# Order of loads and side work in a layer kernel: later gains on half of h, temporaries in their own buffers, last gated block turned beside the down projection

## The chip, the cores and the metric

The kernel runs on one core of a Trainium2 chip (trn2). The metric is the device time of one execution in microseconds (us); lower is better. Each kernel is run several times, and the median counts. One further execution is profiled: the span, the rows and the busy times below are from that one.

## The reference

One layer with float32 inputs: x is 256 tokens of 2048 channels.

```
u = rms_norm(h, g_pre_mix)
proj = u @ w_in                                   # 2048 -> 5120
...   attention, convolution and recurrent groups, each normalised: mixed, 2048 wide
h = h + rms_norm(mixed @ w_out, g_post_mix)       # 2048 -> 2048
u = rms_norm(h, g_pre_ffn)
f = silu(u @ w_gate) * (u @ w_up)                 # 2048 -> 5632, twice
h = h + rms_norm(f @ w_down, g_post_ffn)          # 5632 -> 2048
```

rms_norm divides each token by its root mean square and multiplies channel by channel with a gain g. Products have float32's precision: each operand is split into a high part of the type fp32r and a low part, and three products (high by high, high by low, low by high) are added.

## The kernel before, in words

**Weights.** All weights go through one list, `stream`, of items. A standard item is 256 rows by 512 columns of a matrix (512 KB, `std`). Its way is: a DMA on SP's queue into a raw buffer (`load`, L252), a cast on ACT that makes the high part (`prep`, L274), a subtraction on DVE that makes the low part (L276), then the products on PE. Raw buffers are lent from the shelf `weights`: four (`NRAW`) at first, and three more, `xplaces[0]` to `xplaces[2]`, once the buffers in which x lay are free. There are five pairs of high and low tiles (`NPARTS`). When PE's products with an item have been written down, `release` counts it as done, and `top_up_one` prepares the next items for which a pair is free and then loads as many as it can, up to `AHEAD` = 6 items in front of the one prepared. The queues of PE, ACT and DVE keep the order in which the program writes their instructions. What SP and POOL issue is DMAs, each queue in its own order.

**Products.** A standard item makes 12 products of 512 columns (L333 to L335 in `product`, L326 to L328 in `six`): two halves of its rows, two token halves, three products each. In the feed-forward part the first 512 rows of a gate and an up block (items c0 and c1 of both, four quarters) are multiplied by a scheme of seven products of quarters in place of eight (`seven_in_turn`: P1, P6, P7, Q5, P2, R4, Q3), for all blocks but the first. An item of this scheme makes 6 products of 512 columns; its weights and its operands are sums of quarters, which DVE makes (`sums`, L259, for the weights; `forms` for h and f). P1, P6 and P7 are added up in one bank, and after each of the three ACT copies the value that the bank then holds (`ffn_after`, L1397), before PE may go on adding.

**Side work.** A `Side` job is a generator. After each item of the products one slot (`slot`) lets the jobs write down ACT, DVE and PE work for which their share has been saved up; `need(job)` runs slots until the job is done, which places all its work ahead of what follows.

**From h to the first gate.** The output projection's result makes h, four blocks of 512 channels by two token halves. `h_part` (L1099) adds it up, `h_turn` (L1105) transposes it on PE, `h_hi` (L1112 on DVE for blocks 2 and 3, and the cast L1115 on ACT) and `h_lo` (L1119, DVE) make the parts of it that PE multiplies. The first gate block runs in between, and the calls of `release` in that stretch say where the next weights' casts stand among this work. `h_job` then sums the squares of h on ACT (`squares`, L461), and the root of the mean follows. For blocks 0 and 1 of h the gain g_pre_ffn is not in h at first: the weights of the first gate and up block are multiplied by it instead (`late`, L270, L271). Later `regain_job(b)` multiplies h's block b by the gain: it adds high and low part (L1255, DVE), scales four quarters on ACT (L1258) and splits the result again (`split`: L1235 on ACT, L1236 on DVE); for b = 0 the operands of the seven products (`hform`) follow. Its temporaries h and s lie in `xplaces[0]` to `xplaces[2]`, and these go to the weights' shelf when it ends. Both jobs are added in front of the feed-forward loop, and the first product of block 1's gate asks for both (`side.need(*regain)` in `ffn_bank`). h is saved to memory by POOL's queue ahead of that (`hsave`, L1222).

**The feed-forward loop.** Eleven column blocks of 512; per block the gate items, then the up items. Block 0 has eight of each, c0 to c7; blocks 1 to 10 have the items c2 to c7 and the seven products of two blocks. P1, P6 and P7 of block i + 1 stand among the last up items of block i. When a gate block is complete `silu_job` makes its sigmoid (L1283) and gate values (L1286); `up_job` makes the gated values (L1294, L1295, L1299), transposes them on PE (L1306) and splits them into `fh` and `fl`, and for the four blocks in `SFORM` (1, 3, 5, 7) sends operands of the seven products to memory (`fsave`, L1323).

**The down projection.** After the loop `side.need(last_up)` writes down all that is left of the last block's `up_job`; then POOL loads the eight `fsave` tiles back (L1480), and `downs` runs: six standard items first, then items of seven products mingled with standard ones. `run` is the loop of both: bank, `six`, then `after`, `slot` and `release`.

Of the kernel before, what the change touches and what calls it, by code (L numbers as in the profile page):

```python
# [16 lines left out]
P = 128  # L17
D = 2048
S = 256
# [172 lines left out]
def block_kernel(ctx, tc, xT, x_tok, params, w_in, w_out, w_gate, w_up, w_down, lru_w, g_post, g_post2, out):  # L192
# [30 lines left out]
    for i in range(NFB):  # L223
        g, u = ([std(w[i, c], i=i, col=n, c=c, gains=None if i else late(c)) for c in range(2 if i else 0, 8)] for n, w in ((0, w_gate), (1, w_up)))
        if i:
            q = sevens[i]
            ffn += [*g[:2], q["Q5"], g[2], q["P2"], *g[3:5], q["R4"], g[5], q["Q3"]]
        if i == 0:
            q = sevens[1]
            ffn += [*u[:6], q["P1"], u[6], q["P6"], u[7], q["P7"]]  # L230
        elif i + 1 < NFB:
            q = sevens[i + 1]
            ffn += [*u[:-4], q["P1"], u[-4], q["P6"], *u[-3:-1], q["P7"], u[-1]]
        else:
            ffn += u
# [10 lines left out]
    at = {"load": 0, "prep": 0, "use": 0, "done": 0}  # L246
# [36 lines left out]
    def load_next():  # L283
        while at["load"] in early:
            at["load"] += 1
        i = at["load"]
        if i < min(len(stream), at["prep"] + AHEAD) and len(weights.free) >= len(stream[i].loads):
            load(i)
            at["load"] += 1
            return True  # L290
        return False

    def top_up_one():
# [10 lines left out]
        while load_next():  # L304
            pass
# [879 lines left out]
    release()  # L1185
# [6 lines left out]
    release()  # L1192
    release()
    r = rows(kh[8:10], [take()])
    for t in range(NT):
        half(acc[t], hidden, t, r)
    for t in range(NT):
        h_turn(t, 3)
        h_hi(t, 3)
        h_lo(t, 3)  # L1200
    for _ in range(5):
        release()
# [18 lines left out]
    for b in range(4):  # L1221
        G.dma_start(out=hsave[b], in_=xt[b])  # L1222
    ffp = ctx.enter_context(tc.tile_pool(name="ffp", bufs=1))
    fh, fl = ([place(ffp, f"f{n}{i}")(4, S, F32R) for i in range(NFB - 2)] +
              [place(xs, f"x1{2 * n + i}")(4, S, F32R) for i in range(2)] for n in range(2))
# [23 lines left out]
    def regain_job(b):  # L1249
# [3 lines left out]
        h = xplaces[b](4, S)  # L1253
# [7 lines left out]
        if b == 0:  # L1261
            s = xplaces[2](8, P)
# [6 lines left out]
            weights.free.append(xplaces[2])  # L1269
        weights.free.append(xplaces[b])  # L1270
# [18 lines left out]
    def up_job(i, acc):  # L1289
# [18 lines left out]
        turned = [b.rearrange("p (c t) -> p c t", c=4) for b in tps]  # L1308
        if i in SFORM:
# [23 lines left out]
    def part_tiles(x, k, t):  # L1333

        return [tuple(f(k + kk)[:, t * P:(t + 1) * P] for f in x) for kk in range(2)]

    def form_tiles(form, n):
        return [tuple(f[:, 2 * n + kk, :] for f in form) for kk in range(2)]
# [8 lines left out]
    def run(seq, uses, bank_of, after, tail=0):  # L1347
# [7 lines left out]
        for n, (item, to, tiles) in enumerate(order):  # L1355
# [5 lines left out]
            six(bank, tiles, ws[item], n == first[to], n == end[to] or item.name in READ, to in read)  # L1361
# [9 lines left out]
    def ffn_uses(item):  # L1371
# [3 lines left out]
        return [((item.i, *to), of_product(item.name, hidden, hform))]  # L1375

    def ffn_bank(item, to):
        if to not in accs:
            i, col, _ = to
            if i == 1 and col == 0:  # L1380
                side.need(*regain)
# [7 lines left out]
    def ffn_after(item, full):  # L1389
# [4 lines left out]
        if item.name == "P7":  # L1394
            dst = p167[i % 2]
        if dst is not None:
# [11 lines left out]
    regain = [side.add(1, regain_job(b)) for b in range(2)]  # L1408
# [65 lines left out]
    side.need(last_up)  # L1474
    spots = [stage[0], xplaces[3], place(hlp, "hl2"), place(hlp, "hl3"),
             *(place(ffp, f"hf{n}", 768) for n in range(2)), place(ffp, "p167"), place(ffp, "s")]
    for n, i in enumerate(SFORM):
        sforms[i] = [spots[2 * n + m](6, P, F32R) for m in range(2)]
        for m in range(2):
            G.dma_start(out=sforms[i][m], in_=fsave[i, m])  # L1480
# [17 lines left out]
    def down_uses(item):  # L1498
# [5 lines left out]
        return [((item.b + to[0], to[1]) if to else (item.b, item.name), of_product(item.name, x, sforms[item.i]))]  # L1504

    def down_bank(item, to):
        b, which = to
        half = b // 2
        if to not in ybanks:
            if item.name and half:  # L1510
                side.need(*yjobs[:2])
# [78 lines left out]
```

## Time and profile before

| what | value |
|---|---|
| time, three runs | 1086.96 us median (1086.84 to 1087.55) |
| time of the profiled execution | 1087.62 us |
| its span | 1085.9 us |
| PE busy | 1056.0 us, 97%, 4718 products |
| DVE busy | 849.8 us, 78% |
| ACT busy | 643.9 us, 59% |
| POOL busy | 21.9 us, 2% |
| DMA | 217.50 MB, 200 GB/s over the span |
| chain that ended last | PE 91%, DVE 3%, ACT 3%, issue 1%, DMA 1% |

The span runs from the first to the last instruction that the profiler recorded; 1.7 us of the execution's time lie around it. PE is TensorE's matmuls, PEld its weight loads, DVE VectorE, ACT ScalarE, POOL GpSimd, SP SyncE; SPq and POOLq are their DMA queues. The busy time of a product counts from its start to its modelled end, and products overlap; the pitch, from one start to the next, is what a product takes of PE's time. In a row of the timeline stand the start, the time, the engine, the line, the operation, what it writes and reads, and in brackets how long the engine had been idle before it and what it had waited for. "issue" is time in which the engine waited for nothing that the profile shows. The granted clock is given in parts of full speed.

### The profile page before, as it was taken

Reading aid. Unit: us, or ns where it says so; the run is one execution under the profiler, and the core shown is the slowest. Engines: PE = TensorE matmul, PEld = TensorE weight load, DVE = VectorE, ACT = ScalarE, POOL = GpSimd, SP = SyncE. Lnnn points to the kernel's source line nnn. Section 1 sums busy time; section 2 is a strip of 40 time slices with the busy share of each in tenths; the row PEclk is TensorE's granted clock in tenths of the full one; section 3 lists DMA queues with packets and bytes.
Section 4 is the critical chain, followed back from the end, with each engine's and each line's share of the span. In section 5 each row is a group of like instructions: output and inputs, shape, how many; then the busy total and the mean of one; then the engine's idle time right before and its main releaser. Section 6 shows DMA issues by size and latency. Waiting matters only on the chain.

```text
span 1085.9 us, 13088 instructions
## 1 busy us (share of the span) xinstructions
PE 1056.0 (97%) x4718; PEld 870.5 (80%) x4718; DVE 849.8 (78%) x1040; ACT 643.9 (59%) x819; POOL 21.9 (2%) x43
## 2 busy tenths in 40 slices
PE   8999999999999959999999999999999999999996
PEld 6788888888888748888888888888888788888885
DVE  5576998986687767888788788787786588888885
ACT  5778757678854655565556555555554355555562
POOL 0000001010000000000000000000000000000000
PEclk9999999999999999999999999999999999999998
DMA  8855554556563437566565575567668556646653
GB/s 294 290 185 173 191 175 156 192 171 212 195 234 116 174 118 243 180 207 216 189 224 192 188 232 194 188 210 249 201 200 293 180 194 204 228 172 222 223 191 117
DMA packets 62065, 217.50 MB, mean 200 GB/s; under 512 B 6832, under 2 KB 7216, under 8 KB 62000
## 3 DMA queue, kind: packets, MB, share of 16 engines
q1 hardware_dynamic: 58544, 206.18, 56.9%
q0 software_dynamic: 3456, 10.49, 2.8%
q8 instruction: 37, 0.61, 0.2%
q14 instruction: 28, 0.23, 0.1%
HBM read 209.30 MB, written 7.34 MB: 200 GB/s over the span
## 4 chain that ended last, share of the span: by engine, by line
PE 91%; DVE 3%; ACT 3%; issue 1%; DMA 1%; SPq 0%; DVEq 0%; ACTq 0%
PE acc L327 17%; PE acc L326 17%; PE acc L328 17%; PE acc L333 9%; PE acc L334 9%; PE acc L335 9%; PE bank L326 3%; PE bank L327 3%; PE bank L328 3%; DMA w<-xT 1%; DVE lo L276 1%; PE bank L1306 1%; PE bank L485 1%; ACT hi L274 1%; ACT junk L461 0%
## 5 line engine op out<-in xcount | busy, mean ns | idle before, releaser
L276 DVE TENSOR_TENSOR lo<-w,hi 128x1024 fp32r<-128x1024 f32 x419 | 509.2, 1224 | 188.6 <-ACT hi L274 181.0
L274 ACT CAST hi<-w 128x1024 fp32r<-128x1024 f32 x419 | 436.4, 1051 | 315.5 <-PE acc L328 136.7
L326 PE MATMUL acc<-hi,w 128*128 128x512 f32 x820 | 322.7, 394 | 8.1 <-issue 6.1
L327 PE MATMUL acc<-lo,w 128*128 128x512 f32 x820 | 321.7, 392 | 3.2 <-DVE lo L276 3.2
L328 PE MATMUL acc<-hi,w 128*128 128x512 f32 x820 | 321.6, 392 | 0.0
L326 PEld LDWEIGHTS acc<-hi,w 128*128 128x128 f32 x820 | 155.2, 189 | 41.1 <-issue 6.7
L327 PEld LDWEIGHTS acc<-lo,w 128*128 128x128 f32 x820 | 155.3, 189 | 35.7 <-DVE lo L276 3.9
L328 PEld LDWEIGHTS acc<-hi,w 128*128 128x128 f32 x820 | 155.2, 189 | 32.4
L333 PE MATMUL acc<-hi,w 128*128 128x512 f32 x336 | 134.7, 401 | 2.3 <-DVE w L471 1.1
L334 PE MATMUL acc<-lo,w 128*128 128x512 f32 x336 | 132.6, 395 | 1.1 <-DVE lo L276 0.8
L335 PE MATMUL acc<-hi,w 128*128 128x512 f32 x336 | 132.6, 395 | 0.0
L259 DVE TENSOR_TENSOR w<-w 128x1024 f32<-128x1024 f32 x72 | 87.7, 1218 | 0.0
L333 PEld LDWEIGHTS acc<-hi,w 128*128 128x128 f32 x336 | 63.8, 190 | 17.0 <-ACT hi L903 2.7
L334 PEld LDWEIGHTS acc<-lo,w 128*128 128x128 f32 x336 | 63.8, 190 | 15.3 <-DVE lo L276 1.6
L335 PEld LDWEIGHTS acc<-hi,w 128*128 128x128 f32 x336 | 63.7, 190 | 14.7 <-DVE w L1119 1.3
L326 PE MATMUL bank<-hi,w 128*128 128x512 f32 x168 | 65.4, 390 | 0.0
L327 PE MATMUL bank<-lo,w 128*128 128x512 f32 x168 | 65.4, 389 | 0.0
L328 PE MATMUL bank<-hi,w 128*128 128x512 f32 x168 | 65.4, 389 | 0.0
L727 DVE SCALAR_TENSOR_TENSOR w<-u,par,w 128x256 f32<-128x256 f32 x120 | 51.3, 487 | 0.0
L333 PE MATMUL acc<-hi,mh 128*128 128x512 f32 x128 | 50.5, 395 | 0.0
L335 PE MATMUL acc<-hi,ml 128*128 128x512 f32 x128 | 50.0, 390 | 0.0
L334 PE MATMUL acc<-lo,mh 128*128 128x512 f32 x128 | 49.9, 390 | 0.0
(259 smaller groups left out, 792.0 us busy)
## 6 DMA issues: line engine op xcount, KB each, us to landing
w<-w_gate SPq DMA_DIRECT2D x88, 512.0 KB, 3.7
w<-w_up SPq DMA_DIRECT2D x88, 512.0 KB, 4.2
w<-w_down SPq DMA_DIRECT2D x88, 512.0 KB, 4.4
w<-w_in SPq DMA_DIRECT2D x78, 512.0 KB, 3.4
w<-w_out SPq DMA_DIRECT2D x32, 512.0 KB, 3.5
fsave<-w POOLq DMA_DIRECT2D x8, 384.0 KB, 4.7
w<-fsave POOLq DMA_DIRECT2D x8, 384.0 KB, 5.4
w<-x_tok SPq DMA_DIRECT2D x4, 512.0 KB, 6.3
```

The source lines that it names most:

```text
L259: V.tensor_tensor(out=item.bufs[dst], in0=item.bufs[a], in1=item.bufs[b], op=op)
L274: A.copy(out=hi, in_=raw)
L276: V.tensor_tensor(out=lo, in0=raw, in1=hi.bitcast(F32), op=ALU.subtract)
L326: T.matmul(bank, xhi, hi[:, kk, :], start=first and kk == 0, stop=False, skip_group_check=again)
L327: T.matmul(bank, xhi, lo[:, kk, :], start=False, stop=False, skip_group_check=again)
L328: T.matmul(bank, xlo, hi[:, kk, :], start=False, stop=last and kk == 1, skip_group_check=again)
L333: T.matmul(acc, xh(k)[:, ts], hi[:, kk, :], start=first, stop=False)
L334: T.matmul(acc, xh(k)[:, ts], lo[:, kk, :], start=False, stop=False)
L335: T.matmul(acc, xl(k)[:, ts], hi[:, kk, :], start=False, stop=last)
L485: T.transpose(out=b[:, c * P:(c + 1) * P], in_=src[:, t, c * P:(c + 1) * P], identity=ident)
L727: V.scalar_tensor_tensor(out=cy[:, n, :], in0=u[:, n, j:j + S], scalar=pv("dw_conv_w", j * 4 + n), in1=cy[:, n, :], op0=ALU.mult, op1=ALU.add)
L1306: T.transpose(out=b[:, c * P:(c + 1) * P], in_=ss[t][:, c * P:(c + 1) * P], identity=ident)
```

## The change

Four parts:

- `at["ahead"]`: up to the feed-forward part an item is loaded only up to four ahead and one after each prepared item; from there on it is six ahead as before. With it SP's order at the start differs.
- The turn of h: the calls of `release` stand later, so blocks 2 and 3 of h come ahead of some weights. ACT's order from the first cast of block 2 on was cast, weight, cast, two weights, a weight pair with gains, the two casts of block 3, a pair with gains, squares; it is now two casts, two weights, the two casts of block 3, a weight, two pairs with gains, squares.
- The temporaries of `regain_job` lie in `ffp` tiles that are not yet in use (`f_place`), and `xplaces[0]` to `xplaces[2]` go to the weights' shelf as soon as h has been sent to memory. `regain_job(1)` is added only after block 1's P7, and only the items c2 and c3 of block 1 ask for it; these are now last among the items of each block from 1 on. `fh` and `fl` are made when a block is turned.
- `side.need(last_up)` is gone; the reloads on POOL are a side job of their own that waits for the last `up_job`, and the first seven-product item of the down projection asks for it.

```diff
     for i in range(1, NFB):
         sevens[i] = seven_in_turn(w_gate[i, 0], w_up[i, 0], w_gate[i, 1], w_up[i, 1], i=i)
     for i in range(NFB):
-        g, u = ([std(w[i, c], i=i, col=n, c=c, gains=None if i else late(c)) for c in range(2 if i else 0, 8)] for n, w in ((0, w_gate), (1, w_up)))
+        g, u = ([std(w[i, c], i=i, col=n, c=c, gains=None if i else late(c)) for c in ((4, 5, 6, 7, 2, 3) if i else range(8))] for n, w in ((0, w_gate), (1, w_up)))
         if i:
             q = sevens[i]
             ffn += [*g[:2], q["Q5"], g[2], q["P2"], *g[3:5], q["R4"], g[5], q["Q3"]]
...
     stream += downs[0] + downs[1]
     early = range(gate0 + 1, gate0 + 1 + NEARLY)
     parts = {}
-    at = {"load": 0, "prep": 0, "use": 0, "done": 0}
+    at = {"load": 0, "prep": 0, "use": 0, "done": 0, "ahead": NRAW}
 
     def load(i, raw=None):
         item = stream[i]
...
         while at["load"] in early:
             at["load"] += 1
         i = at["load"]
-        if i < min(len(stream), at["prep"] + AHEAD) and len(weights.free) >= len(stream[i].loads):
+        if i < min(len(stream), at["prep"] + at["ahead"]) and len(weights.free) >= len(stream[i].loads):
             load(i)
             at["load"] += 1
             return True
...
                 return False
             prep(i)
         at["prep"] += 1
-        while load_next():
+        while load_next() and at["ahead"] > NRAW:
             pass
         return True
 
...
     h_part(0, 3)
     h_lo(0, 2)
     h_part(1, 3)
-    release()
     half(acc[1], hidden, 1, r[4:7])
     h_turn(1, 2)
     half(acc[1], hidden, 1, r[7:])
     h_hi(1, 2)
     h_lo(1, 2)
     release()
-    release()
-    release()
     r = rows(kh[8:10], [take()])
-    for t in range(NT):
-        half(acc[t], hidden, t, r)
+    half(acc[0], hidden, 0, r)
     for t in range(NT):
         h_turn(t, 3)
+    half(acc[1], hidden, 1, r)
+    release()
+    for t in range(NT):
         h_hi(t, 3)
+    for t in range(NT):
         h_lo(t, 3)
-    for _ in range(5):
+    for _ in range(7):
         release()
 
     def h_job():
...
 
     for b in range(4):
         G.dma_start(out=hsave[b], in_=xt[b])
+    weights.free.extend(xplaces[:3])
+    at["ahead"] = AHEAD
     ffp = ctx.enter_context(tc.tile_pool(name="ffp", bufs=1))
-    fh, fl = ([place(ffp, f"f{n}{i}")(4, S, F32R) for i in range(NFB - 2)] +
-              [place(xs, f"x1{2 * n + i}")(4, S, F32R) for i in range(2)] for n in range(2))
+    fh, fl = {}, {}
+
+    def f_place(n, i):
+        return place(xs, f"x1{2 * n + i - NFB + 2}") if i >= NFB - 2 else place(ffp, f"f{n}{i}")
+
     both = place(ffp, "s")(NT, CB)
     ss = [both[:, t, :] for t in range(NT)]
     sums_f = both.rearrange("p t c -> p (t c)").rearrange("p (k t) -> p k t", t=P)
...
 
         while ("used", b) not in st:
             yield WAIT
-        h = xplaces[b](4, S)
+        h = f_place(b, 7)(4, S)
         yield 1.2, 0, 0
         V.tensor_tensor(out=h, in0=hh[b].bitcast(F32), in1=hl[b].bitcast(F32), op=ALU.add)
         yield 0, 2.0, 0
...
         yield 1.2, 1.05, 0
         split(hh[b], hl[b], h)
         if b == 0:
-            s = xplaces[2](8, P)
+            s = f_place(0, 8)(8, P)
             yield 1.9, 0, 0
             forms(s, *quarters(h))
             yield 1.0, 0.9, 0
             split(*hform, s[:, 2:8, :])
             yield 0.5, 0.4, 0
             split(hh[0][:, 0:2, P:], hl[0][:, 0:2, P:], s[:, 0:2, :])
-            weights.free.append(xplaces[2])
-        weights.free.append(xplaces[b])
 
     two = place(ffp, "p167")(2, CB)
     p167 = [two[:, 0, :], two[:, 1, :]]
...
+        fh[i], fl[i] = (f_place(n, i)(4, S, F32R) for n in range(2))
...
-        return [tuple(f(k + kk)[:, t * P:(t + 1) * P] for f in x) for kk in range(2)]
+        return lambda: [tuple(f(k + kk)[:, t * P:(t + 1) * P] for f in x) for kk in range(2)]
...
-            six(bank, tiles, ws[item], n == first[to], n == end[to] or item.name in READ, to in read)
+            six(bank, tiles(), ws[item], n == first[to], n == end[to] or item.name in READ, to in read)
...
     def ffn_bank(item, to):
+        if item.i == 1 and item.name is None and item.c < 4:
+            side.need(regain[1])
         if to not in accs:
             i, col, _ = to
             if i == 1 and col == 0:
-                side.need(*regain)
+                side.need(regain[0])
             if i:
                 side.need(*(added[n] for n in ((i - 1, 0),) if n in added))
                 while col and ("up", i - 1) not in st:
...
         dst = {"P1": p1, "P6": p16, "Q5": q5}.get(item.name)
         if item.name == "P7":
             dst = p167[i % 2]
+        if (i, item.name) == (1, "P7"):
+            regain.append(side.add(0, regain_job(1)))
         if dst is not None:
             A.copy(out=dst, in_=accs[(i, 1, 1) if item.name == "Q5" else (i, 0, 1)])
         if item.name == "Q5":
...
                     added[j, col] = side.add(0, job(j, [accs[j, col, t] for t in range(NT)]))
 
     added[0, 0] = side.add(0, silu_job(0, acc))
-    regain = [side.add(1, regain_job(b)) for b in range(2)]
+    regain = [side.add(1, regain_job(0))]
     run(ffn, ffn_uses, ffn_bank, ffn_after)
     last_up = added[NFB - 1, 1]
 
...
 
 
     sforms = {}
-    side.need(last_up)
     spots = [stage[0], xplaces[3], place(hlp, "hl2"), place(hlp, "hl3"),
              *(place(ffp, f"hf{n}", 768) for n in range(2)), place(ffp, "p167"), place(ffp, "s")]
-    for n, i in enumerate(SFORM):
-        sforms[i] = [spots[2 * n + m](6, P, F32R) for m in range(2)]
-        for m in range(2):
-            G.dma_start(out=sforms[i][m], in_=fsave[i, m])
+
+    def sforms_job():
+        yield 0, 0, 0
+        while last_up in side.jobs:
+            yield WAIT
+        for n, i in enumerate(SFORM):
+            sforms[i] = [spots[2 * n + m](6, P, F32R) for m in range(2)]
+            for m in range(2):
+                G.dma_start(out=sforms[i][m], in_=fsave[i, m])
+
+    sforms_ready = side.add(1, sforms_job())
     ff = of(fh, fl)
     NLAST = 4
     kept = {}
...
         to = {"P2": (0, 0), "Q3": (1, 0), "R4": (0, 1)}.get(item.name)
         four = [k for k in range(4 * item.i, 4 * item.i + 4)]
         x = [lambda k, f=f: f(four[k]) for f in ff]
-        return [((item.b + to[0], to[1]) if to else (item.b, item.name), of_product(item.name, x, sforms[item.i]))]
+        return [((item.b + to[0], to[1]) if to else (item.b, item.name), of_product(item.name, x, lambda: sforms[item.i]))]
 
     def down_bank(item, to):
         b, which = to
         half = b // 2
         if to not in ybanks:
-            if item.name and half:
-                side.need(*yjobs[:2])
+            if item.name:
+                side.need(*(yjobs[:2] if half else [sforms_ready]))
             if half == 0 and isinstance(which, int):
                 ybanks[b, 0], ybanks[b, 1] = acc_pair()
             elif half == 1 and not isinstance(which, int):
```

The first place is the start, SP's queue: `xT` is x, turned, by quarters of the channels (the first two in pieces), `w_in` the first weights. Before:

```order
L252 DMA w_179<-w_in 128x1024
L465 DMA w_148<-xT 128x512
L252 DMA w_182<-w_in 128x1024
L252 DMA w_192<-w_in 128x1024
L252 DMA w_194<-w_in 128x1024
L252 DMA w_196<-w_in 128x1024
L465 DMA w_204<-xT 128x1024
```

and now:

```order
L252 DMA w_179<-w_in 128x1024
L465 DMA w_148<-xT 128x512
L252 DMA w_182<-w_in 128x1024
L252 DMA w_192<-w_in 128x1024
L465 DMA w_200<-xT 128x1024
L252 DMA w_206<-w_in 128x1024
L252 DMA w_212<-w_in 128x1024
```

The third quarter of x stood behind four weights in a row and stands behind two now; the rest follows in the same alternation.

The second place is ACT's queue from the end of the first regain to the copies of block 1's P1, P6 and P7 (`w_3001` and `w_3002` are the high parts of h's blocks 0 and 1, the `hi` tiles weights, `par_72` the gains; `w_3477` and `w_3571` are the temporary of `regain_job(1)`, and the copies from `acc` are those of the three, L1397 before and L1405 now). Before:

```order
L1235 CAST w_3001<-w_3434 128x2x128
L1258 ACTIVATE w_3477<-w_3477,par_72 128x256 x4
L274 CAST hi_3501<-w_3461 128x1024
L1235 CAST w_3002<-w_3477 128x1024
L274 CAST hi_3525<-w_3410 128x1024
L1397 COPY w_3386<-acc_3531 128x512
```

and now:

```order
L1240 CAST w_3001<-w_3416 128x2x128
L274 CAST hi_3479<-w_3390 128x1024
L274 CAST hi_3497<-w_3388 128x1024
L1405 COPY w_3364<-acc_3501 128x512
L274 CAST hi_3509<-w_3392 128x1024
L274 CAST hi_3527<-w_3421 128x1024
L1405 COPY w_3365<-acc_3501 128x512
L274 CAST hi_3541<-w_3388 128x1024
L274 CAST hi_3561<-w_3463 128x1024
L1405 COPY w_3367<-acc_3501 128x512
L1263 ACTIVATE w_3571<-w_3571,par_72 128x256 x4
L1240 CAST w_3002<-w_3571 128x1024
```

The four scalings and the cast of the second regain stood ahead of the copy of P1, and now stand behind the copy of P7; each copy has two weights' casts ahead of it.

The third place is PE's queue at the end of the feed-forward loop (`bank` takes the transposes, `w_3383` and `w_3361` are the gated values). Before, with the last two up products first:

```order
L327 MATMUL acc_6668<-lo_6824,w_3004 128x512
L328 MATMUL acc_6668<-hi_6823,w_2904 128x512
L1306 MATMUL bank_6932<-ident_73,w_3383 128x128 x4
L1306 MATMUL bank_6937<-ident_73,w_3383 128x128 x4
L326 MATMUL acc_6962<-hi_6841,w_3361 128x512
```

and now:

```order
L326 MATMUL acc_6931<-hi_6875,w_4318 128x512
L327 MATMUL acc_6931<-lo_6876,w_4318 128x512
L328 MATMUL acc_6931<-hi_6875,w_4319 128x512
L1309 MATMUL bank_6978<-ident_73,w_3361 128x128 x4
L1309 MATMUL bank_6983<-ident_73,w_3361 128x128 x4
L326 MATMUL acc_6930<-hi_6893,w_4318 128x512
```

The transposes followed the last up product directly, and now stand behind three items of the down projection, 36 products; in front of these stands the last up product.

## Rows read from the trace of the kernel before

**Rows 1.** The page's slices: PE's busy tenths and its granted clock.

```profile
PE   8999999999999959999999999999999999999996
...
PEclk9999999999999999999999999999999999999998
```

**Rows 2.** Table of stretches: us, busy PE, PEld, DVE, ACT, POOL (instructions), clock, DMA share, GB/s.

```profile
375.00:400.00 25.00, 19.84 (x83) 15.51 (x82) 16.06 (x26) 14.81 (x24) 0.00 (x0) 0.97 0.38 126
400.00:425.00 25.00, 18.94 (x76) 15.02 (x75) 19.11 (x20) 15.06 (x21) 0.00 (x0) 0.82 0.58 187
```

**Rows 3.** PE's waits: for what, us in total, times, longest.

```profile
PE acc L326 <- issue: 6.1, 1, 6.1
PE acc L327 <- DVE lo L276: 3.2, 2, 2.2
PE bank L1306 <- DVE w L1299: 2.3, 1, 2.3
```

**Rows 4.** The start: SP's timeline, the chain that ended last, PE's timeline.

```profile
6.22 8.19 SPq L252 DMA_DIRECT2D w<-w_in  x4
...
14.46 6.07 DMA w<-xT
...
20.54 0.39 PE L335 MATMUL acc<-hi,w 128*128 128x512 f32 x1
...
28.71 0.39 PE L335 MATMUL acc<-hi,w 128*128 128x512 f32 x1
```

**Rows 5.** PE's timeline, the last nine products of the up projection, first and last.

```profile
839.76 0.39 PE L326 MATMUL acc<-hi,w 128*128 128x512 f32 x1
...
841.57 0.39 PE L328 MATMUL acc<-hi,w 128*128 128x512 f32 x1
```

**Rows 6.** Timeline, the turn of h and what precedes P1.

```profile
358.57 1.22 DVE L276 TENSOR_TENSOR lo<-w,hi 128x1024 fp32r<-128x1024 f32 x1
...
359.71 0.69 DVE L1112 TENSOR_TENSOR w<-bank,par 128x512 f32<-128x512 f32 x1
...
360.43 0.62 ACT L1115 CAST w<-w 128x512 fp32r<-128x512 f32 x1 [2.21 <-DVE w L1112]
...
368.85 1.33 ACT L270 ACTIVATE hi<-w,par 128x512 fp32r<-128x512 f32 x2
...
370.09 0.62 ACT L461 ACTIVATE junk<-w 128x512 f32<-128x512 f32 x1
...
390.87 1.99 ACT L274 CAST hi<-w 128x1024 fp32r<-128x1024 f32 x2
...
391.96 0.49 PE L326 MATMUL acc<-hi,w 128*128 128x512 f32 x1 [1.99 <-ACT hi L274]
```

**Rows 7.** Timeline, ACT and PE ahead of P6.

```profile
399.40 0.40 ACT L1235 CAST w<-w 128x256 fp32r<-128x256 f32 x1
...
402.25 1.70 ACT L1258 ACTIVATE w<-w,par 128x256 f32<-128x256 f32 x4 [2.46 <-DVE w L1255]
...
406.69 0.57 ACT L1397 COPY w<-acc 128x512 f32<-128x512 f32 x1
...
407.36 0.77 PE L326 MATMUL acc<-hi,w 128*128 128x512 f32 x1 [6.06 <-issue]
```

**Rows 8.** Table of stretches, behind the resumption at 407.36.

```profile
407.40:412.20 4.80, 4.80 (x12) 3.79 (x13) 4.76 (x5) 3.29 (x4) 0.00 (x0) 0.50 0.83 294
```

**Rows 9.** PE's timeline, the end of the gates.

```profile
844.22 1.29 PE L1306 MATMUL bank<-ident,w 128*128 128x128 f32 x8 [2.26 <-DVE w L1299]
...
845.27 0.47 PE L326 MATMUL acc<-hi,w 128*128 128x512 f32 x1
...
849.22 0.39 PE L327 MATMUL acc<-lo,w 128*128 128x512 f32 x1
```

**Rows 10.** The page's DMA issues: KB each, median us to landing.

```profile
w<-w_up SPq DMA_DIRECT2D x88, 512.0 KB, 4.2
...
w<-fsave POOLq DMA_DIRECT2D x8, 384.0 KB, 5.4
```

More of the change, by code (lines that the diff above doesn't have):

```diff
@@ L1333, in part_tiles @@
     def part_tiles(x, k, t):
-        return [tuple(f(k + kk)[:, t * P:(t + 1) * P] for f in x) for kk in range(2)]
+        return lambda: [tuple(f(k + kk)[:, t * P:(t + 1) * P] for f in x) for kk in range(2)]
     def form_tiles(form, n):
-        return [tuple(f[:, 2 * n + kk, :] for f in form) for kk in range(2)]
+        return lambda: [tuple(f[:, 2 * n + kk, :] for f in form()) for kk in range(2)]
     def of_product(name, x, form):
@@ L1374, in ffn_uses @@
         to = {"P2": (0, 0), "Q3": (1, 0), "Q5": (1, 1)}.get(item.name, (0, 1))
-        return [((item.i, *to), of_product(item.name, hidden, hform))]
+        return [((item.i, *to), of_product(item.name, hidden, lambda: hform))]
     def ffn_bank(item, to):
+        if item.i == 1 and item.name is None and item.c < 4:
+            side.need(regain[1])
         if to not in accs:
```

## Prediction, made before the changed kernel ran

> **What bounds the kernel now.** I read the slices first: PE is busy in nine tenths or more of nearly all of them, and at the full granted clock in nearly all [rows 1]. So the span is a row of products with a few holes, and a change is worth what it takes out of a hole. The table of stretches finds the widest: 19.84 and 18.94 us busy of 25 in the stretches from 375 and from 400 us, at mean clocks of 0.97 and 0.82 [rows 2]. The list of PE's waits says what ended them: once 6.1 us with no releaser that the profile could name, twice a weight's low part (3.2 us together), and, at another place, L1299's gated value in front of the last transposes (2.3) [rows 3]. A small hole lies at the start, between 20.54 and 28.71 us [rows 4].
>
> The pitch of products at full clock is 0.226 us: eight steps from 839.76 to 841.57 [rows 5]. A standard item is 12 products, 2.7 us; one of the seven is 6, 1.4 us.
>
> **Start: the later half of x goes ahead of two weights.** SP issues in its own order. Before, four weight loads took it 8.19 us from 6.22 on, since some waited for a raw buffer; only then, at 14.46, went the third quarter of x, which landed 6.07 later, at 20.53 [rows 4]. Now it stands behind two of these four. Spread evenly, the second ends at about 10.3 (an estimate from that row), and x lands at about 16.4, well before PE asks for it, at 20.77. From 20.54 to 28.71 PE made 27 steps in 8.17 us; at 0.226 they are 6.1. So at most **2.0 us** come back, and nothing if other transfers come late in its place. I take 1.9: the four microseconds won are twice the hole.
>
> The same edit, one load after each prepared item, leaves the rest of the first 340 us alone: every load still waits for the item that held its buffer, four back, and SP has the same loads in the same places. I cost it at nothing; the four raw buffers cover it.
>
> **The turn of h: the chain that leads to P1 starts earlier.** In front of P1 of block 1 stands one long chain on ACT and DVE: squares of h (from 370.09), root, sigmoid, gate values, first regain, P1's high part, which lets PE go on at 391.96 after a wait of 1.99 [rows 6]. From the first square to P1 that is 21.9 us, in the same order now as before, and nothing in it is removed. Its start moves. DVE made a weight's low part at 358.57 (1.22 us) before it came to L1112 at 359.71, and ACT's cast of the result stood until 360.43 [rows 6]. Now L1112 follows at 358.6 and the cast ends at 359.9. Then ACT has two weight casts (1.99 for two) to 361.9; DVE ends the second low part at 363.2 and two L1112 (0.69 each) at 364.6; ACT's second cast of that pair (0.62) ends at 365.2, one more weight cast at 366.2, two pairs with gains (1.33 each) at 368.8: there the squares start, in place of 370.09. So P1 comes **1.3 us** earlier. PE itself gets through the turn earlier too, but that buys a longer wait before P1, not time. Bounds: 0 (another wait in that chain) and 1.5.
>
> **Behind P1: the second regain leaves ACT's way.** P6 adds into the bank that P1 left, so it waits until ACT has copied P1's value. ACT's order was: a small cast at 399.40 (0.40), the four scalings of the second regain, which stood 2.46 for DVE (402.25, 1.70), a weight cast, the regain's cast, a weight cast, then the copy at 406.69 (0.57); PE resumed at 407.36, 0.1 later [rows 7]. This is the 6.1 that has no releaser. Now only two weight casts stand between the small cast and the copy: 399.80 + 1.99 + 0.57 + 0.1 = 402.5. So P6 starts **4.9 us** earlier, beside the 1.3 above. The most is the whole wait, 6.1; the least is 0, if the casts for c7 or P7 wait for their weights. These are loaded into the buffers freed early, as soon as the squares are done with them; the squares stand at the head of the 21.9 us chain, and a load takes some 4.2 [rows 10].
>
> The regain comes back behind the copy of P7. Its four steps are 1.2 + 1.7 + 1.0 + 1.2 = 5.1 us. Who waits for it is c2 of block 1's gate, which now stands behind c4, c5, Q5, c6, P2 and c7: 60 products, 13.6 us. That is the cover, and it exists only because c2 and c3 were put last; by itself their order moves nothing. Temporaries in another place cost nothing either.
>
> **The end of the gates: the last turn beside the down products.** The last up product is issued at 841.57; PE's next entry is the transposes at 844.22, 2.42 us late, and then, from 845.27 to 849.22, ten products take 3.95 us where 2.26 would do: 1.7 lost to a low clock [rows 5, 9]. In the new order the transposes stand behind three down items, 36 products or 8.2 us, and the gated values that they wait for come within 2.7 of the last up product. The three use blocks 0 and 2, long ready. The eight reloads on POOL come behind this, 5.4 us each from issue to landing [rows 10]; the seventh down item is the first that needs one, 16 us in. So **4.1 us** come back; 2.4 if the clock falls all the same.
>
> **Sum.** 1.9 + 1.3 + 4.9 + 4.1 = 12.2 us. The profiled execution took 1087.62, so 1075.4 for one like it; the median of the runs shown is 1086.96, 0.66 below, and the forecast on that scale is **1074.8**.
>
> **The clock.** After P6 the clock was at 0.50, its lower level of 1.2 GHz, for 4.8 us [rows 8]: 11 products, each 0.22 dearer, 2.4 us. It had fallen behind a run of waits and came back in unbroken work. I leave this loss in, since waits stand before P6 now too. PE was done with c6 at 401.3 (407.36 less 6.06); 1.3 earlier is 400.0, and P6 starts at 401.2 (402.5 less 1.3), so 1.2 us of slower products before P6 would not be felt.
> The Trainium skill ("TensorE: Matmul & The Clock Gate", section "HAM oscillation — how this bites in real kernels") speaks against the change here: waits of some microseconds between short groups of products put the array back to half rate each time, and the wait before P1 gets longer. By that rule all of c6 runs at half rate, up to 12 x 0.226 = 2.7 us dearer; 1.2 of it vanish as said, so its sum would lie between 1074.8 and 1076.3.
>
> **Rivals.**
> - *The clock comes back before P6* (chance 0.14). If it falls at P1 and rises again in c6's unbroken products, the 2.4 us of [rows 8] go too: 1072.4.
> - *The P6 stall only moves* (0.14): weights for c7 or P7 late, or the regain late for c2. For it: SP issues in order, so the load into the first x buffer, which waits for the squares, holds P1's weight behind it. Against it: nearly two thirds of the chain come after the squares. The 4.9 are lost: 1079.7.
> - *Start and turn give nothing* (0.08), as other transfers or casts take the place of those moved: 12.2 less 3.2 is 9.0, so 1078.0.
> - *Slower: the clock stays low* (0.03). Place: P6 to the end of block 1's gate, some 120 products. If all run at the lower level, 109 more than before at 0.226 each, they cost 24.6 us: 1099.4. It decides the sign from 54 products on (12.2 / 0.226). Against it: before, unbroken work brought the clock back within 4.8 us.
> The section of the Trainium skill named above shows a kernel whose clock fell back in every round; no run here shows that.
> - *No change* (0.03): the moved work lies off the path, 1087.0. Against it: the 6.1 us wait ends with ACT's copy to within 0.1.
>
> **How the numbers follow.** The forecast has 0.58, from 1073 to 1077. A measurement of this kernel tells 0.2% (2.2 us) from no change. Faster: 0.58 + 0.14 + 0.14 + 0.08 = 0.94; same 0.03; slower 0.03. The upper bounds, 2.0 + 1.5 + 6.1 + 4.4 (the last with transposes at full clock), make 1073.0; with most of the 2.4 the range starts at 1071.0. It ends at 1079.7.
>
> **What would show it.** In the profile after: no wait of PE between 20 and 29 us; P1 still behind a wait for ACT's cast, longer than 2.0; the 6.1 entry gone from PE's waits, or under 2; the last transposes without a wait and behind down products. It would be wrong if a new wait of over 2 us stood before P6, c2 or the first down items, or if the clock in the stretch from 400 us were below 0.82.

## The result and the profile after

The changed kernel takes 1072.21 us (median of 4 runs, 1072.03 to 1073.17), the kernel before 1087.26 (4 runs, 1086.84 to 1088.43): ratio 0.9862, 95% interval 0.9845 to 0.9879, 15.0 us less. The forecast was 1074.8 with a range from 1071.0 to 1079.7; the result lies inside the range, but below the 1073 to 1077 that the main forecast was given. The profiled execution took 1072.03, with a span of 1070.3.

The page of the kernel after, PE's busy tenths and its granted clock:

```profile
PE   8999999999999989999999999999999999999996
...
PEclk9999999999999989999999999999999999999998
```

The one weak slice of [rows 1], a 5, is an 8 now, and its clock is the one 8 in the middle. The table of stretches (us, busy time of PE, PEld, DVE, ACT and POOL with instructions, clock, DMA share, GB/s):

```profile
375.00:400.00 25.00, 19.82 (x68) 14.49 (x67) 18.74 (x28) 15.07 (x22) 0.00 (x0) 0.80 0.42 137
400.00:425.00 25.00, 25.00 (x116) 20.77 (x115) 22.04 (x23) 16.44 (x22) 0.00 (x0) 1.00 0.65 211
388.00:398.20 10.20, 8.42 (x18) 5.40 (x18) 9.83 (x14) 5.45 (x8) 0.00 (x0) 0.51 0.17 51
```

Against [rows 2] the second stretch is whole. In the first, PE is as busy as before with 68 products in place of 83, since the slow products lie here now: 18 of them between 388 and 398.2, at 0.51. PE's waits (for what, us in total, times, longest):

```profile
PE acc L326 <- ACT hi L274: 3.4, 1, 3.4
PE acc L327 <- DVE lo L276: 1.8, 2, 0.9
PE acc L333 <- DVE w L471: 1.5, 1, 1.5
```

Of [rows 3], the 6.1 without a releaser and the 2.3 in front of the transposes are gone. The longest now is P1's, 3.4 where it was 1.99 [rows 6]. The timeline of the kernel after, at the places of [rows 4 to 9]:

```profile
8.60 0.68 SPq L465 DMA_DIRECT2D w<-xT  x1
...
16.43 1.71 ACT L473 ACTIVATE w<-w,par 128x256 fp32r<-128x256 f32 x4 [0.21 <-DMA w<-xT]
...
26.57 0.39 PE L333 MATMUL acc<-hi,w 128*128 128x512 f32 x1
...
366.06 0.62 ACT L461 ACTIVATE junk<-w 128x512 f32<-128x512 f32 x1
...
384.15 1.71 ACT L1263 ACTIVATE w<-w,par 128x256 f32<-128x256 f32 x4 [3.74 <-DVE w L1260]
...
387.93 0.61 PE L326 MATMUL acc<-hi,w 128*128 128x512 f32 x1 [3.41 <-ACT hi L274]
...
397.56 0.57 ACT L1405 COPY w<-acc 128x512 f32<-128x512 f32 x1
...
397.67 0.63 PE L328 MATMUL acc<-hi,w 128*128 128x512 f32 x1
398.23 0.56 PE L326 MATMUL acc<-hi,w 128*128 128x512 f32 x1
...
830.27 0.39 PE L328 MATMUL acc<-hi,w 128*128 128x512 f32 x1
...
838.67 1.03 PE L1309 MATMUL bank<-ident,w 128*128 128x128 f32 x8
839.46 0.48 PE L326 MATMUL acc<-hi,w 128*128 128x512 f32 x1
```

Both kernels make the same products in the same number, so the start of the n-th can be compared: the lead of the kernel after, us. The last column gives what was gained since the row before that has an entry.

| product | before | after | lead | gained on the way |
|---|---|---|---|---|
| the 76th (third quarter of x well in use) | 28.94 | 26.57 | 2.4 | start 2.4 |
| at the end of the turn of h | 370.06 | 364.64 | 5.4 | |
| first of P1 | 391.96 | 387.93 | 4.0 | turn 1.7 |
| first of P6 | 407.36 | 398.23 | 9.1 | second regain 5.1 |
| in c7, both at full clock | 414.73 | 403.43 | 11.3 | clock 2.2 |
| last up product | 841.57 | 830.27 | 11.3 | |
| last of the products compared | 1075.21 | 1059.65 | 15.6 | end of the gates 4.3 |

### The profile page after: what moved, and what is told of

Same layout as the page of the kernel before. It is cut to its first block, busy times and chain, and to the rows that moved or that the text cites. A ratio compares the mean times of both kernels' runs of the same rounds, so it can differ in the third digit from the quotient of the medians.

```text
span 1070.3 us, 13089 instructions
## 1 busy us (share of the span) xinstructions
PE 1051.6 (98%) x4718; PEld 869.6 (81%) x4718; DVE 848.5 (79%) x1040; ACT 643.8 (60%) x819; POOL 21.8 (2%) x43
## 4 chain that ended last, share of the span: by engine, by line
PE 97%; DVE 1%; ACT 0%; issue 0%; DMA 0%; SPq 0%; DVEq 0%; ACTq 0%
PE acc L327 17%; PE acc L328 17%; PE acc L326 17%; PE acc L334 10%; PE acc L335 10%; PE acc L333 10%; PE bank L326 3%; PE bank L328 3%; PE bank L327 3%; PE bank L1309 1%; PE bank L485 1%; DVE w L1477 0%; PE bank L1105 0%; PE bank L795 0%; PE bank L846 0%
```

## The experiments

Four kernels each undo one part of the change, to see whether the gains of the table are each part's own. All are compared with the changed kernel's 1072.2; the kernel before stood at 1087.4 in those runs. In the later experiments it stood at 1087.6 and 1087.4. The changed kernel was not run again beside any of them, so differences of a few tenths say little. The traces have a noise of their own: by the 18th product, ahead of all that is changed but the start, one profiled execution is up to 1.8 us later than another. Where this matters it is taken off.

**The start undone.**

```diff
-    at = {"load": 0, "prep": 0, "use": 0, "done": 0, "ahead": NRAW}
+    at = {"load": 0, "prep": 0, "use": 0, "done": 0, "ahead": AHEAD}
```

> The changed kernel, with six loads ahead from the start on (the third quarter of x behind four weights again). Additive theory: PE's products get 2.25 us later by 28 us and stay so to the end, 1072.2 + 2.25 = 1074.5. Rival (the start's gain is taken up by a later wait, h's chain ending on something else): within 0.5 of 1072.2.

Measured: 1075.27 (1074.56 to 1075.82), 3.1 slower; in the traces the 74th product is 2.6 later and the end 2.9. SP's queue and ACT's first use of the third quarter:

```profile
6.32 7.86 SPq L252 DMA_DIRECT2D w<-w_in  x4
14.23 0.42 SPq L465 DMA_DIRECT2D w<-xT  x1
```
```profile
20.45 1.71 ACT L473 ACTIVATE w<-w,par 128x256 fp32r<-128x256 f32 x4 [4.65 <-DMA w<-xT]
```

The quarter goes 5.6 us later (14.23 for 8.60) and ACT starts on it 4.0 later. Nothing downstream takes the loss up. The loss is more than the 2.25 that was expected.

**The turn of h undone.**

```diff
     h_part(1, 3)
+    release()
     half(acc[1], hidden, 1, r[4:7])
...
     release()
+    release()
+    release()
     r = rows(kh[8:10], [take()])
-    half(acc[0], hidden, 0, r)
-    for t in range(NT):
-        h_turn(t, 3)
-    half(acc[1], hidden, 1, r)
-    release()
-    for t in range(NT):
-        h_hi(t, 3)
-    for t in range(NT):
-        h_lo(t, 3)
-    for _ in range(7):
+    for t in range(NT):
+        half(acc[t], hidden, t, r)
+    for t in range(NT):
+        h_turn(t, 3)
+        h_hi(t, 3)
+        h_lo(t, 3)
+    for _ in range(5):
         release()
```

> The changed kernel, with the releases in the turn of h where they stood. Additive theory: P1 of block 1 comes 1.8 us later and nothing else moves, 1074.0. Rival (the clock): with the turn undone PE's wait before P1 is about 2.0 again in place of 3.4, the clock stays up through P1 and falls only in c6, so that P6 and what follows run at 0.5 of the clock; 1.8 plus 2 to 5 us, 1076 to 1079.

Measured: 1074.67 (1074.13 to 1075.47), 2.5 slower, 2.1 in the traces. The first square is at 368.24 in place of 366.06, and P1 2.2 later; nothing is lost behind it. But 0.5 of this was lost by the 18th product already, so the turn's own part is about 1.6 in the traces, as in the table. So the rival falls, and its reason with it: P1's wait is 2.0 again, as before the change, but the clock did not stay up until c6. The table of stretches has it low from 392.4 on, 2.3 us behind P1's start, and up again ahead of P6, which starts at 400.40:

```profile
390.10:392.30 2.20, 1.25 (x4) 0.84 (x5) 2.16 (x4) 0.90 (x1) 0.00 (x0) 0.98 0.00 0
392.40:399.20 6.80, 5.33 (x13) 3.71 (x12) 6.50 (x9) 3.45 (x5) 0.00 (x0) 0.51 0.23 77
```

**The second regain ahead of P6 again.**

```diff
-        if (i, item.name) == (1, "P7"):
-            regain.append(side.add(0, regain_job(1)))
...
-    regain = [side.add(1, regain_job(0))]
+    regain = [side.add(1, regain_job(b)) for b in range(2)]
...
-                side.need(regain[0])
+                side.need(*regain)
```

> The changed kernel, with the second regain's work ahead of the copy of P1 again, all else as changed. P1 as in the changed kernel (wait of 3.4). If the regain's 5.1 us in front of the copy are the whole of it: P6 5.1 later, 1077.3. If the earlier return of the clock hangs on this part too (a 5 us wait before P6 leaves the clock low behind it): another 1.9, 1079.2.

Measured: 1080.02 (1078.94 to 1081.66), 7.8 slower, more than the regain's own 5.1. The timeline in front of P6, and the table of stretches before and behind the wait:

```profile
404.45 0.57 ACT L1403 COPY w<-acc 128x512 f32<-128x512 f32 x1
...
405.12 0.77 PE L326 MATMUL acc<-hi,w 128*128 128x512 f32 x1 [7.32 <-issue]
```
```profile
395.30:397.80 2.50, 2.50 (x11) 1.71 (x10) 2.19 (x3) 1.35 (x2) 0.00 (x0) 1.00 0.61 208
405.20:411.20 6.00, 6.00 (x14) 4.74 (x15) 5.96 (x6) 3.25 (x4) 0.00 (x0) 0.50 0.53 184
```

P6 is 5.1 later by its own wait (the profiled execution, the slowest of the four, had lost 1.8 more among its first 18 products). The clock had come back in c6; in the wait it fell again, and 14 products behind it cost 2.7. So the earlier return of the clock in the changed kernel belongs to this part: without the long wait in front of P6 there is nothing for the clock to fall in a second time.

**The wait for the last turn restored.**

```diff
     sforms = {}
+    side.need(last_up)
```

> The changed kernel, with the wait for the last block's turn in front of the down projection again. Theory: 2.4 us of waiting, ten products and the transposes at half clock, 4.6 us in all, 1076.8. Rival (the clock falls in the first down products all the same, so only the wait counts): 2.4, 1074.6.

Measured: 1076.24 (1074.54, 1076.17, 1076.31, 1076.52), 4.0 slower. The profiled execution is the fastest of the four. The timeline at the transposes and the table behind them:

```profile
832.72 1.29 PE L1309 MATMUL bank<-ident,w 128*128 128x128 f32 x8 [2.26 <-DVE w L1302]
833.76 0.47 PE L326 MATMUL acc<-hi,w 128*128 128x512 f32 x1
```
```profile
834.00:838.00 4.00, 4.00 (x20) 3.26 (x19) 1.67 (x4) 1.64 (x2) 0.71 (x2) 1.00 0.89 300
```

The wait is that of [rows 9] to the hundredth, 2.26, and yet the clock stayed up. From the last up product to the end this execution loses 2.7 us: 2.4 of waiting, and 0.25 because the transposes take 1.04 to the next product in place of 0.79. That is not the clock: it was granted at 1.00 while they ran (832.60 to 833.80), as it was in the kernel before (844.20 to 845.20). The same kernel was profiled a second time.

> The kernel of u4_last_turn_waited once more, for a second profile: its first profiled execution was the fastest of four (1074.54), with the clock up behind the wait of 2.3 us, and the others were at 1076.2 to 1076.5. Theory: the clock falls behind this wait in some executions and not in others; in a slower one ten or so products behind the transposes have a pitch of 0.43 (1.7 to 2.2 us in all), in another like the first none has. Rival (the slower executions lose their time at another place): 1076 or more, with all products of that stretch at 0.23.

Measured: 1074.69, again a wait of 2.26, and again 20 products in 4 us at 1.00. The 2.7 us of wait and transposes are thus shown twice. That the other three executions lost their further 1.6 to 2.0 to the clock is likely: the mean granted clock over the span, which is on record for every execution, was 0.992 in the fastest and 0.990 in those three, and 0.002 of 1073 us is 2.1 us (an estimate, 1 to 3 by the rounding). Where in the kernel they lost it no profile shows. In the kernel before, the loss behind this wait is in [rows 9].

**c2 and c3 first again.**

```diff
-... for c in ((4, 5, 6, 7, 2, 3) if i else range(8))] ...
+... for c in (range(2 if i else 0, 8))] ...
```

> The changed kernel, with c2 and c3 first again in blocks 1 to 10. Theory: the second regain behind P7 is free only since c2 comes late. In the changed kernel its high part ends at 410.4 and its low part at 411.7, while the first gate item of block 1 starts at 403.9: with c2 there PE waits 6.5 us, 1078.7, and up to 2.7 more if the clock falls in the wait, 1081.4. Rival (the order of the items does nothing, since another item's weights could be taken meanwhile): within 1 of 1072.2.

Measured: 1081.76 (1081.06 to 1083.63), 9.6 slower. PE's timeline at block 1's first gate item and the table of stretches behind it:

```profile
410.77 0.80 PE L326 MATMUL acc<-hi,w 128*128 128x512 f32 x1 [6.51 <-ACT w L1240]
```
```profile
411.00:416.00 5.00, 4.96 (x12) 3.42 (x13) 2.12 (x2) 0.67 (x1) 0.00 (x0) 0.54 0.00 0
```

A wait of 6.51 and the clock behind it, the upper end of what was expected. Without the new order the part that gained 5.1 and brought the clock back would have lost all of that. That the order by itself moves nothing was not run.

**Products that keep PE awake.** Three kernels put extra products, whose result is read by nobody, into PE's waits (`FILL` says how many in front of which item; here the first kernel's):

```diff
+            if seq is ffn and n and order[n - 1][0] is not item:
+                for _ in range(FILL.get((item.i, item.name or item.c), 0)):
+                    T.matmul(filler, hh[3][:, 0, :P], hh[2][:, 0:2, :], start=True, stop=True, skip_group_check=True)
...
+    FILL = {(1, 'P1'): 15}
+    filler = banks.lend()
...
```

The first: the changed kernel, 15 in front of P1.

> The changed kernel with 15 products whose result nobody reads in front of P1, in PE's wait of 3.4 us, so that PE is not idle there. Theory: the clock stays up through P1 and c6, but P6 still starts when ACT has copied P1 (398.2), so the 17 slow products in front of it cost nothing: within 0.7 of 1072.2. Rival (the slow products are part of what sets the end, and the clock matters in itself): 0.2 for each of those behind the last wait in c6, 2.0 us, 1070.2.

Measured: 1073.62 (1071.46, 1072.52, 1074.72, 1074.81), 1.4 slower, which neither theory nor rival expected. In the profiled execution, the fastest, the clock stays up through P1 but falls in c6, behind a wait of 2.20:

```profile
388.00:393.00 5.00, 1.96 (x7) 1.34 (x8) 4.93 (x8) 1.12 (x2) 0.00 (x0) 1.00 0.00 0
394.00:396.00 2.00, 2.00 (x6) 1.54 (x5) 1.70 (x2) 2.00 (x3) 0.00 (x0) 0.50 0.63 240
398.00:402.00 4.00, 4.00 (x19) 3.29 (x18) 4.00 (x4) 2.84 (x4) 0.00 (x0) 1.00 0.59 205
```

P6 is 0.5 earlier and so was already the 18th product: the rival's 2.0 don't come, and in this execution the filling neither gains nor costs. What the two executions at 1074.8 lost was not seen. In one of them the mean granted clock was 0.995 against 0.993 in the profiled one, so there it was not the clock.

The second: 15, 3 in front of c6 and 16 in front of P6.

> The same with 3 more such products in front of c6 and 16 in front of P6, so that every wait of PE between c5 and P6 is short. Theory: clock up throughout, P6 still at 398.2 by ACT's copy, within 0.7 of 1072.2. If the wait in front of P6 that the first filling opens brings a new fall of the clock, this one is faster than the first by up to 2.4.

Measured: 1073.58 (1072.99 to 1075.27), 1.4 slower, outside the 0.7 as well. The clock is at 1.00 in every stretch of 4 us from 384 to 404. But the filling was too long: ACT's copy ends at 398.54 and the 16 extra products only at 399.9, so P6 is 1.7 late, 0.4 of it from the start, and the end is 1.5 late. From P6 on, the clock kept up throughout brings 0.2 here. Whether a filling of the right length would bring more was not run.

The third: the kernel before, with 8, 9 and 28.

> The kernel before the change, with 8 such products in front of P1, 9 in front of c6 and 28 in front of P6, each somewhat less than the wait there. Theory: the clock does not fall, P6 still starts at 407.4 by ACT's copy, and the 11 products behind it take 0.23 in place of 0.43: 2.4 us faster than the kernel before, 1085.0. Rival (these products are slow for another reason, the weight transfers at a DMA share of 0.83 beside them): no change, 1087.4.

Measured: 1086.01 against 1087.56 (10 and 13 runs), ratio 0.9981, interval 0.9971 to 0.9990. The median is between theory and rival. In the traces P6 is 1.0 late (408.32; 0.7 of it stems from the start), and 2.3 us are won from there to c7 and kept to the end, where 2.4 were expected. The table of stretches behind P6:

```profile
408.00:412.00 4.00, 3.68 (x16) 3.08 (x17) 4.00 (x5) 2.92 (x5) 0.00 (x0) 1.00 0.83 267
```

The DMA share is the 0.83 of [rows 8], where the clock was 0.50: the transfers did not slow these products, the clock did. This is the most direct price of the clock behind P6, since P6 itself moves little.

**What holds P6 and P1 now.** Three kernels go on from the changed one. The first moves the casts for c7 and P7 behind P1's copy:

```diff
+                if seq is ffn and (item.i, item.col if item.name is None else 0, item.name or item.c) in ((0, 1, 4), (0, 1, 5)):
+                    continue
-                release()
+                for _ in range(3 if seq is ffn and (item.i, item.name) == (1, "P1") else 1):
+                    release()
```

> The changed kernel, with the casts for c7 and P7 of ACT written behind the copy of P1 in place of in front of it. The copy is then ready at about 396.3 in place of 398.1. Theory: in the changed kernel both the copy and c6's slow products (0.43 each, last start 397.67) stand in front of P6, so moving the copy alone gives nothing, within 0.7 of 1072.2. Rival (the copy alone holds P6): 1.9 faster, 1070.3.

Measured: 1071.63 (1071.37 to 1072.02), 0.6 faster, of which 0.2 were there before P1. The copy comes 2 us earlier and P6 starts right behind c6's slow products all the same:

```profile
395.45 0.58 ACT L1408 COPY w<-acc 128x512 f32<-128x512 f32 x1
...
397.46 0.44 PE L328 MATMUL acc<-hi,w 128*128 128x512 f32 x1
...
397.74 0.40 PE L326 MATMUL acc<-hi,w 128*128 128x512 f32 x1
```

Of the 0.5 by which P6 is earlier, 0.2 were there before P1, so the copy's 2 us gave 0.3. In the changed kernel two things end together in front of P6, the copy (398.13) and c6's slow products. Taking away either alone gives little: this kernel takes away the copy, and in the first filling c6 is done sooner and P6 waits for the copy (0.63).

The second lets the first regain's sum and scalings go ahead of the wait for c1, since they only read h:

```diff
-        while ("used", b) not in st:
-            yield WAIT
         h = f_place(b, 7)(4, S)
...
             A.activation(h[:, n, :], h[:, n, :], AF.Copy, scale=pv("g_pre_ffn", 4 * b + n))
+        while ("used", b) not in st:
+            yield WAIT
```

> The changed kernel, with the first regain's sum and its four scalings ahead of c5's weight on DVE and ACT (they only read h, so they need not wait until PE is done with c1). Theory: the chain squares, root, sigmoid, regain sets P1 and P6, and its scalings, at 384.15 behind a wait of 3.7, can start at 379.5. c5 then waits some 1.5 us for its weight, P1 starts at about 386, and P6, held by DVE's queue and ACT's copy, at about 396.5: 1.7 faster, 1070.5. Rival (c5's wait and a fall of the clock eat it): 1072.2 or slower.

Measured: 1070.38 (1069.85 to 1070.95), 1.8 faster. The profiled execution is the slowest of the four and had lost 1.0 by the 18th product; all the same its P6 is 1.0 earlier. P6 waits, and the wait ends with the copy: now the copy is last.

```profile
396.59 0.58 ACT L1405 COPY w<-acc 128x512 f32<-128x512 f32 x1
...
397.27 0.47 PE L326 MATMUL acc<-hi,w 128*128 128x512 f32 x1 [1.90 <-issue]
```

> Both edits. Theory: with the chain earlier the copy of P1 is the last wait in front of P6, so here the second edit counts: P6 at about 394.6, 3.6 faster than the changed kernel, 1068.6. Rival (the two edits act on the same wait): as the first of them alone, 1070.5.

Measured: 1069.47 (1068.99 to 1070.12), 2.7 faster than the changed kernel where 3.6 were expected, and its ratio to the kernel before is 0.9833 (0.9818 to 0.9847), where the changed kernel has 0.9862 (0.9845 to 0.9879). These intervals overlap; the runs of the two kernels do not. It is the fastest version of this study. Its timeline and its table of stretches:

```profile
388.29 0.50 PE L327 MATMUL acc<-lo,w 128*128 128x512 f32 x1 [2.12 <-DVE lo L276]
...
391.42 0.50 PE L327 MATMUL acc<-lo,w 128*128 128x512 f32 x1 [1.48 <-DVE lo L276]
...
393.55 0.58 ACT L1408 COPY w<-acc 128x512 f32<-128x512 f32 x1
...
394.23 0.47 PE L326 MATMUL acc<-hi,w 128*128 128x512 f32 x1
```
```profile
375.00:400.00 25.00, 20.18 (x83) 14.80 (x82) 20.40 (x30) 15.36 (x23) 0.00 (x0) 1.00 0.44 146
```

P6 is 4.0 earlier than in the changed kernel, and the clock is at 1.00 throughout. Of the 4.0, 0.5 goes again in P6, which waits for a low part, and 0.8 in c4, whose second half adds into the bank of P7 and waits for the copy of P7 (401.73, 0.57 long; the product starts at 402.36). That copy has two casts ahead of it which stood 1.42 for DVE. What holds P1 and c6 here is DVE: both waits of PE end with a low part, and DVE goes from one instruction to the next with hardly a pause from 381.83 to 392.8.

## Why the prediction was right, and where it was off

The signs that were named came: no wait of PE between 20 and 29 us, P1 behind a wait of 3.41 for ACT's cast, the 6.1 gone, the last transposes without a wait. None of the signs against it did: no new wait of over 2 us, and a clock of 1.00 in the stretch from 400 us. The four parts were right in their mechanism and each came out somewhat larger than its term; the clock was judged wrongly.

**Start** (1.9 taken, 0 to 2.0): 2.4. The third quarter was issued at 8.6 and in use from 16.43, where 10.3 and 16.4 had been estimated; the hole between 20 and 29 us is gone. The bound counted PE's steps from 20.54 on. The lead was 0.3 by the 18th product already, which is within the noise of the traces there, so the hole itself gave about 2.0.

**Turn** (1.3 taken, 0 to 1.5): 1.7. The squares start at 366.06, 4.0 earlier, of which 2.4 stem from the start. The sum added up durations, but on ACT the next instruction starts about 0.1 before the one ahead has ended by the profile: the weight cast at 362.65 is 1.05 long and the next starts 0.95 behind it, the two pairs with gains take 2.46 from start to start where 2.66 had been reckoned. P1's wait got longer, as said.

**Second regain** (4.9 taken, 0 to 6.1): 5.1. The weights for c7 and P7 were not late, and c2 did not wait for its operand: the cover was there, and the kernel with c2 first shows what it is worth.

**End of the gates** (4.1 taken, 2.4 to 4.4): 4.3, made of the wait of 2.4, 0.25 at the transposes (0.8 from their start to the next product's, for 1.05 in [rows 9]) and 1.7 of the clock. The upper bound's "transposes at full clock" is a wrong reading: the clock was at 1.00 during the transposes before the change too, and in the kernel with the wait restored they take 1.04 at 1.00 too; they lose the 0.25 where they start behind a wait. The two profiles with the wait restored show that the clock's share was not certain: the kernel before had lost it in its profile, those two did not.

**The clock** is the step that failed. The prediction left the loss of [rows 8] in, 2.4 us, "since waits stand before P6 now too", and gave its return a chance of 0.14. It returned. Between the profiled executions the gain is 15.6 us, 3.4 above the sum; 2.2 of the 3.4 are this term, and the four above share the rest. The prediction counted the waits in front of P6 but did not ask which of them the clock would fall behind. It fell at P1, behind the longer wait, and 18 products ran at 0.51, as the Trainium skill ("TensorE: Matmul & The Clock Gate", section "HAM oscillation — how this bites in real kernels") lets one expect of short groups of products between waits. All of c6 was slow, but it filled the time until ACT's copy and cost nothing: P6 started 0.10 behind the copy's end (398.13), the same 0.1 as in the kernel before. Then P6 ran on without a pause, and its pitch was 0.23 again from 398.63 on. The kernel with the second regain put back shows the other case: clock up in c6, a wait of 7.3, and 14 products at 0.50 behind it. And the kernel before with its waits filled wins 2.3 behind P6 with the clock alone.

The result is nearly the rival's 1072.4, in part by luck: the rival let the clock rise within c6, where it rose only at P6, and the four parts gave 1.2 more than their sum in the traces. The gain by the medians is 15.0, by the traces 15.6.

The example in that section of the Trainium skill has longer waits than the 2.26 in front of the transposes. This one cost the clock in one profile and not in two others, so a shorter wait can cost it but need not.

The other rivals did not come: the stall did not move, start and turn gave what they should, the clock did not stay low, and there was a change. The medians of the four undone parts sum to 3.1 + 2.5 + 7.8 + 4.0 = 17.4, above the 15.0 of all together. The runs of one of these kernels spread by up to 2.7 us. In the traces, less what each execution had lost or won ahead of the part in question, the four sum to 2.9 + 1.6 + 7.8 + 2.7 = 15.0, where the whole change has 15.6; the 1.7 of the clock at the end of the gates are in the whole and not in these four.

## What to carry to other kernels

When an edit removes a wait, ask what the clock did behind that wait: here the low clock went with it, and that was worth 2.2 us beside the wait's 5.1. Slow products that end no later than another engine's result cost nothing in this kernel, and keeping PE busy in front of them gained nothing; what counted was the clock of the products behind the last wait. Work that is put off needs its cover named: without the order of six items the kernel lost 9.6 us, more than the 7.3 that the part which it protects had brought.

## What was not expected of the hardware

The clock's fall is not set by the wait in front of it alone. Three further stretches of the kernel before:

```profile
392.00:398.50 6.50, 3.33 (x12) 2.25 (x13) 6.43 (x10) 1.75 (x3) 0.00 (x0) 1.00 0.30 95
398.60:407.30 8.70, 2.71 (x7) 1.60 (x5) 5.70 (x7) 6.24 (x11) 0.00 (x0) 0.70 0.36 113
...
845.30:849.20 3.90, 3.90 (x12) 3.07 (x11) 1.77 (x3) 0.76 (x2) 0.92 (x2) 0.56 0.95 305
```

Behind the same wait before P1 (1.99 and 1.97) the granted clock fell 6.6 us after P1's start in the kernel before (1.00 until 398.5) and 2.3 us after it in the kernel with the turn undone. Up to 2.3 us behind P1's start both had the same waits, the second of 0.95; the kernel before then had one more, of 2.21, and still ran at full clock for 1.2 us behind it. Behind waits of 2.12 and 1.48 in the fastest version it did not fall at all. The wait of 2.26 in front of the transposes was followed by 0.56 in one profile, from 845.30 to 849.20 of the kernel before, and by 1.00 in two others. What else decides it, these runs don't tell. Times of single executions of one kernel, 1074.54 at a mean clock of 0.992 beside 1076.52 at 0.990, may be its trace.
